# Fewer accumulating DMAs, later weight sums and other banks for two turns in a two-layer decoder kernel

## The chip, the cores and the metric

The kernel runs on one core of a Trainium2 chip. The metric is the time of one execution on the device in microseconds, here the median of several runs. A core has five engines that run beside each other: TensorE (PE in the profile, its weight loads PEld), VectorE (DVE), ScalarE (ACT), GpSimd (POOL) and SyncE (SP). Each works off its own queue of instructions in order; semaphores order the queues against each other. Sixteen DMA engines move data; DMAs are issued here from SP (plain loads) and from POOL (loads that add to what is there already, called accumulating).

## The reference

Two layers over 512 tokens of width 1024, all in float32. A layer is a half-weighted SwiGLU network, a mixer (windowed attention and a short convolution behind one projection), and another half-weighted SwiGLU network:

```python
def rms_norm(x, gain):
    inv = lax.rsqrt(jnp.mean(x * x, axis=-1, keepdims=True) + NORM_EPS)
    return x * inv * gain

def swiglu(h, w_gate, w_up, w_down):          # 1024 -> 2816 -> 1024
    return (jax.nn.silu(h @ w_gate) * (h @ w_up)) @ w_down

for l in range(2):
    x = x + 0.5 * swiglu(rms_norm(x, ffn1_norm[l]), ffn1_wg[l], ffn1_wu[l], ffn1_wd[l])
    h = rms_norm(x, mix_norm[l])
    z = h @ w_in[l]
    ...
    x = x + concat([attn_out, conv_out]) @ w_out[l]
    x = x + 0.5 * swiglu(rms_norm(x, ffn2_norm[l]), ffn2_wg[l], ffn2_wu[l], ffn2_wd[l])
return rms_norm(x, final_norm)
```

So there are four feed-forward networks in a run. The change touches them only.

## The kernel before

**Products in three parts.** Each operand of a product is split into a high part, rounded to a short float32 form (`fp32r`), and a low part, the rest: `wh`, `wl` for weights, `xh`, `xl` or `ah`, `al` for activations. A product is three matmuls for each piece: high x high, low x high, high x low.

**How a weight tile is split.** A tile (512 KB, 128 x 1024) is loaded by SP into one of 8 `raw` buffers (line 174), and then, by `split` (lines 189 to 191), ScalarE casts it to `wh` and VectorE makes `wl = raw - wh`. There is a second way, `"far"` (lines 224 to 228): ScalarE writes `wl = -raw` (L226) and casts `wh = raw` (L227) and a DMA from POOL's queue adds `raw` onto `wl`. Since `wl` and `wh` have three buffers each, a tile's split starts when the product three tiles before it is done. Splits are made in the order of the list `order`, two products ahead (`SPLIT_AHEAD`); `plan` fills that list, and a tile in it has a word for how it is made.

**A network's stages.** The 22 column tiles of the hidden width are taken in blocks of two. The lists `FIRST` (first network), `INNER` (the two in the middle) and `LAST` name the stages. In the last three:

- `("p", 0)`: block 0's two gate and two up tiles by plain products, 24 matmuls each (L255, L258, L262, function `plain`). All four tiles are `"far"` here.
- `("d", (0,))`: block 0's part of the down-projection, two tiles, 48 matmuls in all, `"far"` too.
- `("w", 1)`, `("w", 3)`, ...: a pair of blocks by `winograd2`, a product scheme with seven half-size products instead of eight. It works with sums of weight quarters, made in the buffers: for each of two halves `h` the tiles `a11`, `a12` are loaded, `s1` (`w_up`, two quarters added) and `s3` (`w_up` with `w_gate` added) are loaded with a second, accumulating DMA from POOL (L185), and `a22` is loaded. VectorE makes `s2 = a11 + s1` in `a11`'s buffer (L207) and the last chain's `s4 = a12 + a11` in `a12`'s buffer (L233). The seven chains (`CHAINS`) run in the order a11, a12, s2, s3, s1, a22, s4; each is 48 matmuls (L722), 24 for each half.
- `("d", ...)`: the down-projection of the blocks that are ready.

A chain that starts (`start`) takes two PSUM banks: `x` of the tag `mm` (4 banks), `w` of `aux` (2), `y` of `sc` (2). They are given out in turn. The steps 0, 2, 4 and 6 go to `x`, 1 to `w`, 3 and 5 to `y`.

**Turning.** `winograd2` leaves activations with tokens in the partitions; the down-projection wants them the other way, so four tiles for each pair are transposed on TensorE into a bank of the tag `sc` (L766), read by ScalarE (`ah`) and VectorE (`al`). These turns are kept in `pending` and made by `flush`: within the first three steps of a pair that follows directly, or between the products of a down-projection. A pair follows a pair directly only once in a network: `("w", 1)`, `("w", 3)` in the last three.

**What else VectorE does around block 0.** In the product before it (the mixer's output or a down-projection), VectorE adds each column to `x`, then makes `xl` (L374) and sums squares (L383). During block 0 it scales and sums the normed activations into the operands of the seven chains (`scale`, `make`: b11, b21, t1 to t4, b22).

The order of each engine's instructions is set by a scheduler that plans with costs of its own, not by the order in which the code is written alone.

Of the kernel before, what the change touches and what calls it, by code (L numbers as in the profile page):

```python
# [15 lines left out]
P = 128  # L16
D = 1024
S = 512
# [5 lines left out]
KC = D // P  # L24
NT = S // P
# [14 lines left out]
FORMS = ("a11", "a12", "s2", "s3", "s1", "a22", "s4")  # L40
# [15 lines left out]
def trunk_kernel(  # L56
# [32 lines left out]
    def psum(tag, shape, name):  # L89
        return ps.tile(shape, F32, tag=tag, bufs={"mm": 4, "sc": 2, "aux": 2}[tag], name=name)  # L90
# [69 lines left out]
    order = []  # L160
# [3 lines left out]
    def add_unit(*unit):  # L164
        units.append(unit)
        return len(units) - 1
# [26 lines left out]
    def need_split(g):  # L193
        while state["split"] <= min(g, len(order) - 1):
            n = state["split"]
            u, what = order[n]
            if what in (None, "wide", "far"):
                need_raw(u + LOAD_AHEAD)
                raw = raw_of.pop(u)
            elif isinstance(what, tuple):  # L200

                what, h = what
                last = {"a11": 0, "a12": 4, "s2": 2, "s3": 6, "s1": 2, "a22": 8, "s4": 4}[what]
                need_raw(u + max(last, 4) + h + LOAD_AHEAD)
                a11, s1, a12, s3, a22 = (raw_of.get(u + 2 * i + h) for i in range(5))
                if what == "s2":
                    nc.vector.tensor_add(a11, a11, s1)  # L207
                raw = {"a11": a11, "a12": a12, "s2": a11, "s3": s3, "s1": s1, "a22": a22, "s4": a12}[what]
            else:

                need_raw(u + 4 + LOAD_AHEAD)
                a11, a12, s1, s3, a22 = (raw_of.get(u + i) for i in range(5))
                if what == "s2":
                    nc.vector.tensor_add(a11, a11, s1)
                if what == "s4":
                    nc.vector.tensor_add(a11, a11, a12)
                raw = {"a11": a11, "a12": a12, "s2": a11, "s3": s3, "s1": s1, "a22": a22, "s4": a11}[what]
                if what == FORMS[-1]:
                    for i in range(5):
                        del raw_of[u + i]  # L220
            shape = list(raw.shape)
            hi = wpool.tile(shape, F32R, tag="wh", bufs=3, name=f"wh_{n}")
            lo = wpool.tile(shape, F32R, tag="wl", bufs=3, name=f"wl_{n}")
            if what == "far":

                nc.scalar.activation(lo, raw, AF.Copy, scale=-1.0)  # L226
                nc.scalar.copy(hi, raw)  # L227
                nc.gpsimd.dma_start(out=f32(lo), in_=raw, accum_op=ALU.add)
            elif n:
                split(hi, lo, raw)  # L230
            if isinstance(order[n][1], tuple):
                if what == "s2":
                    nc.vector.tensor_add(a12, a12, a11)  # L233
                done = {"s2": (0,), "s1": (1,), "s3": (3,), "a22": (4,), "s4": (2,)}.get(what, ())
                for i in done:
                    del raw_of[u + 2 * i + h]
            split_of[n] = (hi, lo)
            state["split"] += 1
# [42 lines left out]
    def plan():  # L281
        def cols(src, k0, kc, n, how=None):
            wide = abreast(kc)
            for b in range(0, n, wide):
                order.append((add_unit((src, k0, kc, b * P, wide * P)), how))

        def plain(wg, wu, b, how):
            for w in (wg, wu):
                for j in range(2):
                    order.append((add_unit((w, 0, KC, (2 * b + j) * P, P)), how))  # L290

        def up(wg, wu, b):
            top, low = ((w, k, KC // 2, 2 * b * P, 2 * P) for w, k in ((wu, 0), (wu, KC // 2)))
            first = (wg, 0, KC // 2, 2 * b * P, 2 * P)
            u = add_unit(first)
            add_unit((wg, KC // 2, KC // 2, 2 * b * P, 2 * P))
            add_unit(top, low)
            add_unit(top, first)
            add_unit(low)
            order.extend((u, what) for what in FORMS)  # L300

        def up2(wg, wu, b):
            def at(w, half, h):
                return w, KC // 2 * half + 2 * h, 2, 2 * b * P, S

            u = len(units)
            for what in (
                ((wg, 0),), ((wu, 0), (wu, 1)), ((wg, 1),), ((wu, 0), (wg, 0)), ((wu, 1),)
            ):
                for h in range(2):  # L310
                    add_unit(*(at(w, half, h) for w, half in what))
            order.extend((u, (what, h)) for what in FORMS for h in range(2))

        def ffn(wg, wu, wd, stages):
            for what, b in stages:
                how = "far" if b in (0, (0,)) and stages is not FIRST else None
                if what == "p":
                    plain(wg, wu, b, how)
                if what == "u":
                    up(wg, wu, b)  # L320
                if what == "w":
                    up2(wg, wu, b)
                if what != "d":
                    continue
                if stages is not LAST or b[-1] < FF // (2 * P) - 1:
                    cols(wd, 2 * b[0], 2 * len(b), KC, how)
                    continue
                for half in range(2):
                    for k in range(0, 2 * len(b), 2):
                        u = add_unit((wd, 2 * b[0] + k, 2, half * S, S))  # L330
                        if half == 0:
                            order.append((u, "wide"))

        for l in range(DEPTH):
            ffn(ffn1_wg[l], ffn1_wu[l], ffn1_wd[l], INNER if l else FIRST)
            for c in MIX_COLS:
                for j in range(2):
                    order.append((add_unit((w_in[l], 0, KC, (2 * c + j) * P, P)), None))
            cols(w_out[l], 0, KC, KC)
            ffn(ffn2_wg[l], ffn2_wu[l], ffn2_wd[l], INNER if l + 1 < DEPTH else LAST)  # L340
# [253 lines left out]
    def ffn(norm, stages, after=None, late=None):  # L594
# [4 lines left out]
        def plain(b):  # L599
            gates = []  # L600

            def gate(acc):
                t = g2(f"gate_{norm.i}_{b}_{len(gates)}")
                nc.vector.tensor_mul(t, acc, norm.inv)
                nc.scalar.activation(t, t, AF.Silu)
                nc.vector.tensor_mul(t, t, norm.inv)
                gates.append(t)

            hi, lo = g4(f"ah_{norm.i}_{b}"), g4(f"al_{norm.i}_{b}")

            def up(j, acc):
                t = gates[j]
                nc.vector.tensor_mul(t, acc, t)
                split(hi[:, j, :], lo[:, j, :], t)

            if norm.inv is None:
                accs = norm.groups(4, [opening] if first else [])
                gate(accs[0])
                gate(accs[1])
                norm.scale(stock if first else g4)  # L620
                up(0, accs[2])
                if not first:
                    norm.make("b11")
                up(1, accs[3])
            else:
                accs = [group(norm.h) for _ in range(2)]
                norm.make("b11")
                gate(accs[0])
                accs.append(group(norm.h))
                gate(accs[1])  # L630
                norm.make("b21")
                accs.append(group(norm.h))
                up(0, accs[2])
                norm.make("t2")
                up(1, accs[3])
            acts[b] = (hi, lo)
# [57 lines left out]
        def winograd2(b, between=None):  # L694


            name = f"{norm.i}_{b}"
# [9 lines left out]
            for step, (acc, operand, start) in enumerate(CHAINS):  # L707
# [41 lines left out]
                            nc.scalar.activation(gates[2 + u], out, AF.Silu)  # L749
                            nc.vector.tensor_mul(ups[2 + u], ups[2 + u], gates[2 + u])  # L750

                if step < 3:
                    flush(2 if step == 2 else 1)
                if between:
                    between(step)
                if not first and step < 3:
# [3 lines left out]
            for j in range(2):  # L760
                acts[b + j] = (g4(f"ah_{name}_{j}"), g4(f"al_{name}_{j}"))

            def turn(c):
                tp = psum("sc", [P, S], f"at_{name}_{c}")
                for t in range(NT):
                    nc.tensor.transpose(  # L766
                        tp[:, t * P : (t + 1) * P], ups[t][:, c * P : (c + 1) * P], ident
                    )
                hi, lo = acts[b + c // 2]
                split(hi[:, c % 2, :], lo[:, c % 2, :], tp)  # L770

            pending.extend(lambda c=c: turn(c) for c in range(NT))

        pending = []

        def flush(n=1):
            for _ in range(n):
                if pending:
                    pending.pop(0)()

        end = None
        for i, (what, b) in enumerate(stages):
# [392 lines left out]
```

## Time and profile before

| | |
|---|---|
| Runs | 1734.77, 1739.11, 1740.63 us; median 1739.11 |
| Profiled execution | 1734.7 us, its span 1732.7 us |
| TensorE's granted clock | 0.999 |
| TensorE busy | 1717.6 us (99%) |
| VectorE, ScalarE, GpSimd busy | 1217.9, 850.8, 164.4 us |
| HBM | 229.68 MB read, 2.10 MB written |

The profile is of one execution. Matmuls overlap in the pipe, so that a row's duration (0.39 us) is longer than the step from one start to the next; the step is what counts. In the timeline a row is: start, duration, engine, line, operation, out<-in, and in brackets the idle time before it with what ended it. In the views of waits a row is: who <- for whom: total, times, longest. The three networks with the stages above begin at about 520, 867 and 1376 us of the span.

### The profile page before, as it was taken

The numbers are of one execution on the slowest core, as the hardware profiler recorded it, in microseconds if no ns is written. First come the engines' busy times: TensorE is split into PE (matmuls) and PEld (weight loads), VectorE is DVE, ScalarE is ACT, GpSimd is POOL, SyncE is SP. The second block draws the span as 40 slices with busy tenths as digits, with TensorE's granted clock in tenths as the row PEclk, the third lists the DMA queues.
The fourth block names the chain that finished last, engine by engine and source line by source line (L and its number), as shares of the span: only waits on it lengthen the run. The fifth ranks groups of instructions, "written<-read, shape, count | busy, mean of one in ns | idle before, by whom it ended". The sixth has DMA issues, their size and how long they took to land.

```text
span 1732.7 us, 20824 instructions
## 1 busy us (share of the span) xinstructions
PE 1717.6 (99%) x7922; PEld 1416.9 (82%) x7922; DVE 1217.9 (70%) x1685; ACT 850.8 (49%) x1236; POOL 164.4 (9%) x151
## 2 busy tenths in 40 slices
PE   9999999999999999999999999999999999999998
PEld 7888888988887888888878888888888878888887
DVE  7986666668757966666688666666787498666763
ACT  6544443546545544444465444444564555344353
POOL 1011000001201110110011100100022011100101
PEclk9999999999999999999999999999999999999999
DMA  8467455422437674574377745743124567664541
GB/s 244 107 167 205 130 139 142 131 73 62 119 102 169 171 198 129 136 192 136 110 168 174 198 130 142 183 143 100 50 61 127 129 143 205 162 167 127 144 134 49
DMA packets 202503, 242.57 MB, mean 140 GB/s; under 512 B 7772, under 2 KB 125604, under 8 KB 202404
## 3 DMA queue, kind: packets, MB, share of 16 engines
q1 hardware_dynamic: 176932, 189.46, 35.9%
q0 software_dynamic: 24320, 50.34, 17.1%
q8 instruction: 62, 1.02, 0.2%
q10 hardware_dynamic: 1152, 1.45, 0.2%
q14 instruction: 37, 0.30, 0.1%
HBM read 229.68 MB, written 2.10 MB: 134 GB/s over the span
## 4 chain that ended last, share of the span: by engine, by line
PE 84%; issue 6%; DVE 5%; DMA 4%; ACT 1%; POOL 0%; SPq 0%; POOLq 0%; ACTq 0%; DVEq 0%
PE x L722 22%; PE acc L255 12%; PE acc L258 12%; PE acc L262 12%; PE y L722 12%; PE w L722 5%; DMA wl<-raw 3%; PE at L766 2%; DVE wl L191 2%; DMA raw<-in_ffn_wu_dram 1%; PE end L857 1%; PE end L859 1%; PE end L858 1%; PE x L666 1%; PE pt L1043 1%
## 5 line engine op out<-in xcount | busy, mean ns | idle before, releaser
L190 ACT CAST wh<-raw 128x1024 fp32r<-128x1024 f32 (+2 forms) x415 | 432.8, 1045 | 617.9 <-PE acc L258 219.3
L191 DVE TENSOR_TENSOR wl<-raw,wh 128x1024 fp32r<-128x1024 f32 (+2 forms) x414 | 507.3, 1227 | 231.6 <-ACT wh L190 230.4
L255 PE MATMUL acc<-ah,wh 128*128 128x512 f32 x640 | 254.1, 399 | 0.0
L262 PE MATMUL acc<-ah,wl 128*128 128x512 f32 x640 | 250.0, 391 | 0.0
L258 PE MATMUL acc<-al,wh 128*128 128x512 f32 x640 | 249.1, 389 | 0.0
L805 DVE SCALAR_TENSOR_TENSOR x<-acc,x 128x512 f32<-128x512 f32 x176 | 120.0, 688 | 108.1 <-PE acc L262 107.5
L255 PE MATMUL acc<-xh,wh 128*128 128x512 f32 x448 | 176.5, 394 | 0.1
L258 PE MATMUL acc<-xl,wh 128*128 128x512 f32 x448 | 175.2, 391 | 0.1
L262 PE MATMUL acc<-xh,wl 128*128 128x512 f32 x416 | 163.0, 392 | 5.4 <-DMA wl<-raw 5.4
L262 PEld LDWEIGHTS acc<-ah,wl 128*128 128x128 f32 x640 | 120.1, 188 | 26.0
L258 PEld LDWEIGHTS acc<-al,wh 128*128 128x128 f32 x640 | 120.4, 188 | 23.3
L255 PEld LDWEIGHTS acc<-ah,wh 128*128 128x128 f32 x640 | 120.0, 188 | 23.6 <-ACT ah L190 1.0
L185 POOL DMA_DIRECT2D raw<-in_ffn_wu_dram x39 | 47.1, 1211 | 671.5 <-DVE u L746 343.6
L258 PEld LDWEIGHTS acc<-xl,wh 128*128 128x128 f32 x448 | 84.2, 188 | 18.3 <-DVE xl L374 1.6
L255 PEld LDWEIGHTS acc<-xh,wh 128*128 128x128 f32 x448 | 84.2, 188 | 17.3 <-issue 0.5
L262 PEld LDWEIGHTS acc<-xh,wl 128*128 128x128 f32 x416 | 78.1, 188 | 23.4 <-DMA wl<-raw 7.1
L190 ACT CAST ah<-at 128x512 fp32r<-128x512 f32 x76 | 44.1, 584 | 67.6 <-PE at L766 67.6
L185 POOL DMA_DIRECT2D raw<-in_ffn_wg_dram x39 | 46.9, 1204 | 234.5 <-DMA raw<-in_ffn_wu_dram 153.4
L191 DVE TENSOR_TENSOR al<-at,ah 128x512 fp32r<-128x512 f32 x76 | 51.9, 687 | 15.2 <-ACT ah L190 15.0
L722 PE MATMUL x<-wh,ft1h 128*128 128x512 f32 x152 | 59.7, 392 | 0.2
L722 PE MATMUL y<-wh,ft3h 128*128 128x512 f32 x152 | 59.6, 392 | 0.3
L722 PE MATMUL x<-wh,ft2h 128*128 128x512 f32 x152 | 59.5, 392 | 0.0
(297 smaller groups left out, 3441.0 us busy)
## 6 DMA issues: line engine op xcount, KB each, us to landing
raw<-in_ffn_wu_dram SPq DMA_DIRECT2D x127, 512.0 KB, 3.8
raw<-in_ffn_wg_dram SPq DMA_DIRECT2D x87, 512.0 KB, 4.9
raw<-in_ffn_wd_dram SPq DMA_DIRECT2D x82, 512.0 KB, 3.4
raw<-in_ffn_wu_dram POOLq DMA_DIRECT2D x39, 512.0 KB, 7.6
raw<-in_ffn_wg_dram POOLq DMA_DIRECT2D x39, 512.0 KB, 6.0
raw<-in_w_in_dram SPq DMA_DIRECT2D x36, 512.0 KB, 3.7
wl<-raw POOLq DMA_DIRECT2D x18, 512.0 KB, 7.4
raw<-in_w_out_dram SPq DMA_DIRECT2D x16, 512.0 KB, 4.1
```

The costliest lines, as they stand in the source:

```text
L185: nc.gpsimd.dma_start(out=r, in_=rows_of(*more), accum_op=ALU.add)
L190: nc.scalar.copy(hi, raw)
L191: eng.tensor_sub(lo, raw, f32(hi))
L255: nc.tensor.matmul(acc, hi[:, k, :], rhs[k][0], start=k == 0, stop=False)
L258: nc.tensor.matmul(acc, hi[:, k, :], rhs[k][1], start=False, stop=n == 0 and k == last)
L262: nc.tensor.matmul(acc, lo[:, k, :], rhs[k][0], start=False, stop=k == last)
L666: nc.tensor.matmul(out, w[:, k, cols], x_[:, k, :], start=start and k + i == 0, stop=k == KC // 2 - 1 and i == 2, skip_group_check=not start,)
L722: nc.tensor.matmul(out, x_[:, 2 * h + k, tok], w[:, k, :], start=start and h + k + i == 0, stop=h + k == 2 and i == 2, skip_group_check=no ...
L766: nc.tensor.transpose(tp[:, t * P : (t + 1) * P], ups[t][:, c * P : (c + 1) * P], ident)
L805: nc.vector.scalar_tensor_tensor(xs[c], acc, 0.5, xs[c], op0=ALU.mult, op1=ALU.add)
L857: nc.tensor.matmul(acc, ah[:, tok], wh[:, cols], start=k == 0, stop=False)
L858: nc.tensor.matmul(acc, ah[:, tok], wl[:, cols], start=False, stop=False)
```

## The change

- Block 0's four gate and up tiles are no longer `"far"`: each is split by ScalarE and VectorE as other tiles are. Its two down-projection tiles stay `"far"`.
- In the first pair (`("w", 1)`) the first tile (`a11`, first half) becomes `"far"`.
- The sum `a12 + a11` is issued after the split of `s3` instead of that of `s2`, so `a11`'s buffer is given back there too.
- The two turns made at step 2 of a pair take banks of the tag `mm` instead of `sc`.

In all 18 accumulating DMAs `wl<-raw` become 9.

```diff
@@ need_split
             n = state["split"]
             u, what = order[n]
+            far = what == "far"
...
-                what, h = what
+                what, h, far = what
...
-            if what == "far":
+            if far:
 
                 nc.scalar.activation(lo, raw, AF.Copy, scale=-1.0)
                 nc.scalar.copy(hi, raw)
...
             if isinstance(order[n][1], tuple):
-                if what == "s2":
+                if what == "s3":
                     nc.vector.tensor_add(a12, a12, a11)
-                done = {"s2": (0,), "s1": (1,), "s3": (3,), "a22": (4,), "s4": (2,)}.get(what, ())
+                done = {"s3": (0, 3), "s1": (1,), "a22": (4,), "s4": (2,)}.get(what, ())
@@ plan
-        def plain(wg, wu, b, how):
+        def plain(wg, wu, b):
             for w in (wg, wu):
                 for j in range(2):
-                    order.append((add_unit((w, 0, KC, (2 * b + j) * P, P)), how))
+                    order.append((add_unit((w, 0, KC, (2 * b + j) * P, P)), None))
...
-        def up2(wg, wu, b):
+        def up2(wg, wu, b, far):
...
-            order.extend((u, (what, h)) for what in FORMS for h in range(2))
+            order.extend(
+                (u, (what, h, far and what == "a11" and h == 0)) for what in FORMS for h in range(2)
+            )
...
-                how = "far" if b in (0, (0,)) and stages is not FIRST else None
+                how = "far" if b == (0,) and stages is not FIRST else None
...
-                    up2(wg, wu, b)
+                    up2(wg, wu, b, b == 1)
@@ winograd2
-                if step < 3:
-                    flush(2 if step == 2 else 1)
+                if step < 2:
+                    flush()
+                if step == 2:
+                    flush(2, "mm")
...
-            def turn(c):
-                tp = psum("sc", [P, S], f"at_{name}_{c}")
+            def turn(c, tag="sc"):
+                tp = psum(tag, [P, S], f"at_{name}_{c}")
...
-            pending.extend(lambda c=c: turn(c) for c in range(NT))
+            pending.extend(lambda *tag, c=c: turn(c, *tag) for c in range(NT))
...
-        def flush(n=1):
+        def flush(n=1, *tag):
             for _ in range(n):
                 if pending:
-                    pending.pop(0)()
+                    pending.pop(0)(*tag)
```

## The prediction

> **What bounds the kernel now.** I read the page first, then TensorE's view of waits, then the timeline around each wait.
>
> ```profile
> span 1732.7 us, 20824 instructions
> PE 1717.6 (99%) x7922; PEld 1416.9 (82%) x7922; DVE 1217.9 (70%) x1685; ACT 850.8 (49%) x1236; POOL 164.4 (9%) x151
> ...
> raw<-in_ffn_wu_dram SPq DMA_DIRECT2D x127, 512.0 KB, 3.8
> ...
> wl<-raw POOLq DMA_DIRECT2D x18, 512.0 KB, 7.4
> ```
>
> TensorE (PE) is busy for 99% of the span and the change leaves its work alone, so the only time to win is time in which TensorE stands still or runs stretched. The chain of waits gives the pace of an undisturbed stretch:
>
> ```profile
> 660.12 5.44 PE x L722 x24
> ```
>
> That is 5.44 / 24 = 0.227 us for one matmul of 512 columns; a longer step between two starts is a loss. TensorE's waits, summed over the run:
>
> ```profile
> PE acc L262 <- DMA wl<-raw: 5.4, 3, 2.5
> ...
> PE y L722 <- DVE wl L191: 0.5, 3, 0.2
> ```
>
> Both come three times, once in each of the three feed-forward networks after the first. One is at the last product of block 0's gate and up tiles, which waits for the low part `wl` that an accumulating DMA makes. The other is in the first pair's fourth chain (`y`, weights `s3`). The timeline of TensorE shows the first at its largest:
>
> ```profile
> 537.57 0.39 PE L258 MATMUL acc<-xl,wh 128*128 128x512 f32 x1
> 540.43 0.50 PE L262 MATMUL acc<-xh,wl 128*128 128x512 f32 x1 [2.47 <-DMA wl<-raw]
> 540.77 0.40 PE L255 MATMUL acc<-xh,wh 128*128 128x512 f32 x1
> ```
>
> The start comes 2.86 us after the one before, 2.63 over the pace: 0.16 more than the view's 2.47, and the step behind it (0.34) loses another 0.11. So a wait costs what the view says plus 0.27.
>
> **Block 0's four tiles lose their accumulating DMAs.** Why that DMA is late is in the timelines of GpSimd (POOL) and SyncE:
>
> ```profile
> 530.27 1.20 POOL L185 DMA_DIRECT2D raw<-in_ffn_wu_dram  x1 [6.63 <-DMA raw<-in_ffn_wu_dram]
> 530.99 1.40 POOL L228 DMA_DIRECT2D wl<-raw  x1
> 534.14 0.85 POOL L228 DMA_DIRECT2D wl<-raw  x1 [1.75 <-ACT wl L226]
> ...
> 549.32 1.20 POOL L185 DMA_DIRECT2D raw<-in_ffn_wg_dram  x1 [8.53 <-DMA raw<-in_ffn_wu_dram]
> ```
>
> ```profile
> 543.68 0.37 SPq L174 DMA_DIRECT2D raw<-in_ffn_wu_dram  x1
> ```
>
> ```profile
> DMA to landing us min/median/max: 4.4/7.4/9.5
> ```
>
> POOL's queue is first in, first out. The fourth tile's `wl` DMA stood behind an accumulating load of `w_up` that itself waited 6.63 us for its base load, and then took 9.4 us (530.99 to 540.4). The base load was late because its buffer was still being read by an earlier `wl` DMA. After the change the four tiles are split by a ScalarE cast and a VectorE subtraction, and their raw buffers come free when that subtraction ends instead of when a DMA lands. The wait goes: 5.4 + 3 x 0.27 = 6.2 us.
>
> What this adds is 12 subtractions on VectorE, and what it takes away is 12 negated copies on ScalarE:
>
> ```profile
> 521.40 1.05 ACT L226 ACTIVATE wl<-raw 128x1024 fp32r<-128x1024 f32 x1
> ```
>
> ```profile
> 523.10 0.75 DVE L374 SCALAR_TENSOR_TENSOR xl<-x,par,xh 128x512 fp32r<-128x512 f32 x1 [1.74 <-ACT xh L373]
> ```
>
> In the order of instructions each subtraction stands just ahead of an `xl`, during the product before block 0. There VectorE idles 1.74 us waiting for ScalarE's `xh`, and that `xh` now comes about 1 us sooner because the 1.05 us copy ahead of it is gone. A subtraction (1.22 us, row 565.30 below) fits the gap; cost taken as nothing. If the gap were full, `xl` of the last column would be late; the one above ends at 523.85, and TensorE needs it 21 matmuls (4.8 us) into the next product, at about 525.2: 1.4 us of cover.
>
> **The first pair's first tile and its sums.** One tile in each network goes the other way: its subtraction leaves VectorE for an accumulating DMA. And the sum `a12 + a11`, for the last chain, moves behind the split of `s3`. VectorE's timeline:
>
> ```profile
> 545.75 0.69 DVE L613 TENSOR_TENSOR gate<-acc,gate 128x512 f32<-128x512 f32 x1 [2.71 <-PE acc L262]
> ...
> 565.30 1.22 DVE L233 TENSOR_TENSOR raw<-raw,raw 128x1024 f32<-128x1024 f32 x1
> ...
> 569.31 1.21 DVE L233 TENSOR_TENSOR raw<-raw,raw 128x1024 f32<-128x1024 f32 x1
> ```
>
> From 545.75 VectorE runs without a gap until 580, so everything in its queue up to there is late by what stands ahead of it. The row's 2.71 us of idle shows that it had been waiting for TensorE's stalled product, so it moves forward with it. The stalls it causes are these:
>
> ```profile
> 570.99 0.39 PE L722 MATMUL x<-wh,ft2l 128*128 128x512 f32 x1
> 571.48 0.50 PE L722 MATMUL y<-wh,ft3h 128*128 128x512 f32 x1
> ...
> 574.11 0.39 PE L722 MATMUL y<-wh,ft3l 128*128 128x512 f32 x1
> 574.65 0.50 PE L722 MATMUL y<-wl,ft3h 128*128 128x512 f32 x1 [0.16 <-DVE wl L191]
> ```
>
> 0.49 and 0.54 instead of 0.227, with 0.11 after each: 0.79 us, three times, 2.4 us. The `wl` in question will come 1.2 (the removed subtraction) + 2.4 (two sums) = 3.6 us sooner, well over the lateness. What is late next is `wl` of the fifth chain (`s1`), behind the same sums: only the 1.2 helps it, while TensorE arrives 0.8 sooner. Bounds are 0 and 0.7 us for each network; I take 0.2, near zero because that chain does not wait now: 0.6 us in all. In the other pairs the order of instructions leaves the sums where they were. In the first pair `a22`'s load, which takes `a11`'s buffer, starts later; the page's 3.8 us for such a load stand against four products (4 x 2.72 us) from the split of `s3` to that of `a22`, so I take nothing.
>
> The moved tile's DMA is the part with a price I cannot read off. ScalarE can start its cast only when the fourth tile's product ends (call this T; about 542.8 without the stall), and needs 2.1 us for cast and negated copy; POOL issues it at T + 2.3. The 4.4 to 9.5 us above put the landing at T + 6.7 to T + 11.8. TensorE needs it after block 0's 48 matmuls of down-projection and two of its own: T + 50 x 0.227 = T + 11.4. So cost is 0 to 0.4 us each; I take 0, since the queue is emptier (four fewer such DMAs ahead). The Trainium skill, page "DMA: Bandwidth & Descriptors", section "Anatomy of one DMA — SWDGE (gpsimd) path", fits 2.0 us plus bytes over 436 GB/s; for 512 KB that is an estimate of 3.2 us, by which the cost would be 0 as well, though this trace's minimum is already 4.4.
>
> **Turns through other banks.** When the second pair runs its third chain, the last two transposed tiles of the first pair are turned in the two `sc` banks that the next chain's `y` needs. The order of instructions therefore puts part of the fifth chain first, whose weights are not ready:
>
> ```profile
> 613.57 0.38 PE L766 MATMUL at<-ident,p 128*128 128x128 f32 x2
> 614.03 0.50 PE L722 MATMUL x<-wh,ft1h 128*128 128x512 f32 x1
> ...
> 614.85 0.39 PE L722 MATMUL x<-wh,ft1l 128*128 128x512 f32 x1
> 615.29 0.50 PE L722 MATMUL x<-wl,ft1h 128*128 128x512 f32 x1
> ```
>
> ```profile
> 959.28 0.50 PE L722 MATMUL x<-wh,ft1h 128*128 128x512 f32 x1
> ```
>
> ```profile
> 1469.13 0.50 PE L722 MATMUL x<-wh,ft1h 128*128 128x512 f32 x1
> ```
>
> Two small transposes take 0.22 us, so 0.46 loses 0.24; 0.44 loses 0.21; with 0.11 after each it is 0.67 us, and the other two rows show the same stretched matmul in the other networks: 2.0 us. With `mm` banks `y` comes first, its banks long free. In exchange the next down-projection takes the bank of the pair's own `x` accumulator:
>
> ```profile
> 635.13 0.60 ACT L749 ACTIVATE gate<-x 128x512 f32<-128x512 f32 x1 [0.53 <-PE x L722]
> ```
>
> ```profile
> 636.29 0.39 PE L255 MATMUL acc<-ah,wh 128*128 128x512 f32 x1
> ```
>
> ScalarE is done reading it at 635.73, 0.56 us before the first matmul that would reuse it. Cost nothing; if ScalarE slipped by a whole cast (1.05 us) it would be 0.5 us for each network.
>
> **Sum.** 6.2 + 2.4 + 2.0 - 0.6 = 10.0 us. The profiled execution took 1734.7 us (span 1732.7), so it would become 1724.7. The median of the three runs, 1739.1, lies 4.4 above it; off the median the forecast is 1729.1 us. A difference under 0.3% (5.2 us) can hardly be told from none here.
>
> **Rivals.** (1) POOL's queue holds the moved tile back. In the new order its DMA stands behind the accumulating load of row 549.32, which needs a base load, which needs the buffer of block 0's first down-projection tile (still an accumulating DMA: issued 534.14, buffer free at 543.68). I count on that DMA landing by about 539, alone in the queue. If it keeps its 9.5 us, the load is issued as before at 549.3, the tile's DMA at 550.5, and with 7.4 to 9.5 us it lands at 557.9 to 560.0 against a need at 554.2: 3.7 to 5.8 us for each network, 11 to 17 in all, 1740 to 1746 us. It decides from a landing about 2 us later than I count on. For it: all six `wl` DMAs were slow. Against: what crowded them is what the change removes. Chance 0.11, about half of it slower by over 0.3%.
> (2) VectorE becomes the bound ahead of block 0: four subtractions (4.9 us) against 1.4 us of cover leave up to 3.5 us for each network if none of them finds a gap, 10.5 in all: 1740 us, just above the time before. Against: its idle gaps there, 1.74 us in one column. Chance 0.08.
> (3) The moved tile's DMA is written out late because VectorE is full while GpSimd prepares it: one subtraction of 1.22 us in the way, on top of the 0.4 above, 1.6 each, 4.8 in all, 1734 us. Row 549.32 speaks against: 1.20 us in the midst of the full stretch, like 530.27 before it. The Trainium skill, page "SBUF — State Buffer", section "SBUF: two separate sides", has this rule: a VectorE instruction holding the shared port keeps GpSimd from writing descriptors. Chance 0.04.
> (4) The change does not do what it says on VectorE and the banks: the two shorter waits only move to the next chain, and just 6.2 us go: 1733 us. Chance 0.05.
>
> **How the numbers follow.** The forecast has 0.72. Its own range runs from 1722 (the fastest run, 1734.8, less 10.6 and some 2 us of DMA waits in the other runs that this profile doesn't show) to 1733 (the slowest, 1740.6, less 7.6). To 1738 it takes in cases 3 and 4 and most of 2. Faster by over 0.3%: 0.72 + 0.05 + 0.03 = 0.80; same: 0.05 + 0.06 + 0.01 = 0.12; slower: 0.06 + 0.02 = 0.08.
>
> **What would show it.** Right: no wait of TensorE on `wl<-raw` at L263 (L262 of the code before); VectorE 14 us busier at most; the first pair's chains back to 5.44 us for 24; after the turns 0.227 from the first `y`. Wrong: TensorE waiting at the first pair's first matmuls (`x<-wl,fb11h`) on a DMA says case 1 or 3; waiting for `xl` in block 0's first product says case 2; a wait of the down-projection behind the second pair on ScalarE's `gate` says that the banks only moved the stall.

## The result, and the profile after

The changed kernel takes **1724.0 us** (median of six runs, 1723.67 to 1724.62) against 1739.7 us for six runs of the kernel before beside it (1734.77 to 1742.1). The ratio is 0.9913, 95% interval 0.9899 to 0.9926: faster by 0.9%. The forecast was 1729.1 with a range of 1722 to 1738: the measured time lies inside it, near its lower end. The profiled execution took 1723.67 us, 11.0 less than the one of before; the sum had said 10.0.

From the page of the kernel after:

```profile
span 1721.9 us, 20808 instructions
PE 1713.1 (99%) x7922; PEld 1418.3 (82%) x7922; DVE 1229.7 (71%) x1694; ACT 844.2 (49%) x1227; POOL 156.6 (9%) x142
...
PE 97%; DVE 2%; ACT 1%; issue 0%; ACTq 0%; DVEq 0%
...
wl<-raw POOLq DMA_DIRECT2D x9, 512.0 KB, 5.3
```

VectorE has 11.8 us more to do and ScalarE 6.6 less; neither bounds the kernel, since the chain that ended last (third line) is now TensorE for 97%, where it was 84%. The nine accumulating DMAs `wl<-raw` that are left land in 5.3 us at the median, instead of 7.4. All that TensorE waited for, by its view of waits:

```profile
PE idle L117 <- DVE warm L486: 1.2, 1, 1.2
PE o L1063 <- DVE pl L1052: 0.8, 2, 0.4
PE acc L256 <- ACT ah L190: 0.2, 1, 0.2
```

The first two belong to the kernel's start and the mixer; the third is taken up further down. No row names `wl<-raw`, none names `y`. The chain of waits shows the first four of the first pair's seven chains. Each is 24 matmuls, 12 for each half of its weights (the description of `winograd2` above gives 48 and 24, which is twice too many):

```profile
554.28 5.56 PE x L725 x24
559.84 5.44 PE w L725 x24
565.28 5.44 PE x L725 x24
570.72 5.44 PE y L725 x24
```

The fourth, where `y` stalled before, runs at 5.44 us, the undisturbed pace; the first is 0.12 over it, and that is where the moved tile is needed. The turns, in TensorE's timeline:

```profile
610.25 0.38 PE L771 MATMUL at<-ident,p 128*128 128x128 f32 x2
610.39 0.48 PE L725 MATMUL y<-wh,ft3h 128*128 128x512 f32 x1
610.70 0.40 PE L725 MATMUL y<-wh,ft3l 128*128 128x512 f32 x1
610.94 0.39 PE L725 MATMUL y<-wl,ft3h 128*128 128x512 f32 x1
```

`y` follows the transposes at once: 0.14 after the last two, then steps of 0.31 and 0.24. The first of these loses 0.09 us, where 0.67 was lost before.

**One sum for each profiled execution.** I took each step between two starts of TensorE's matmuls over the whole run, subtracted the undisturbed step of its size (0.227 us for 512 columns, 0.120 for 256, 0.109 for less) and added up what is left. This is the time lost by waits, by stretched steps, and at half clock:

| profiled execution of | lost steps, us | time, us | difference |
|---|---|---|---|
| before, first | 24.0 | 1734.70 | 1710.7 |
| before, again | 28.5 | 1739.26 | 1710.8 |
| after | 13.2 | 1723.67 | 1710.5 |
| tiles only | 18.6 | 1729.11 | 1710.5 |
| no block-0 change, no moved tile | 23.6 | 1734.17 | 1710.6 |
| no block-0 change | 30.1 | 1740.78 | 1710.7 |
| no accumulating DMA | 20.7 | 1731.26 | 1710.5 |

The kernels have the same matmuls, so the difference can only change with what lies ahead of the first matmul, behind the last, or outside the span; it is the same to 0.3 us. The sum is bookkeeping and names no cause, but it says where to look: each loss stands between two rows of TensorE. Over the last three networks together, lost steps fall from 6.6 to 0.0 us around the end of block 0's gate and up products, from 2.7 to 0.2 in the first pair and from 2.4 to 0.3 in the second pair with its turns, and rise from 0.6 to 1.0 in block 0's part of the down-projection. That is all of the 10.8 us between the first row and the third.

### The profile page after: what moved, and what is told of

Its sections match the earlier page's. It is cut to its first block, busy times and chain, and to the rows that moved or that the text cites. A ratio compares the mean times of both kernels' runs of the same rounds, so it can differ in the third digit from the quotient of the medians.

```text
span 1721.9 us, 20808 instructions
## 1 busy us (share of the span) xinstructions
PE 1713.1 (99%) x7922; PEld 1418.3 (82%) x7922; DVE 1229.7 (71%) x1694; ACT 844.2 (49%) x1227; POOL 156.6 (9%) x142
## 3 DMA queue, kind: packets, MB, share of 16 engines
q8 instruction: 62, 1.02, 0.2%
## 4 chain that ended last, share of the span: by engine, by line
PE 97%; DVE 2%; ACT 1%; issue 0%; ACTq 0%; DVEq 0%
PE x L725 24%; PE acc L256 15%; PE acc L259 15%; PE acc L263 15%; PE y L725 12%; PE w L725 6%; PE at L771 2%; PE end L864 1%; PE end L862 1%; PE end L863 1%; PE x L669 1%; PE pt L1048 1%; DVE p L1041 0%; DVE wl L191 0%; ACT p L1033 0%; PE y L669 0%
## 5 line engine op out<-in xcount | busy, mean ns | idle before, releaser
L190 ACT CAST wh<-raw 128x1024 fp32r<-128x1024 f32 (+2 forms) x424 | 443.0, 1045 | 616.1 <-PE acc L259 243.1
L191 DVE TENSOR_TENSOR wl<-raw,wh 128x1024 fp32r<-128x1024 f32 (+2 forms) x423 | 518.5, 1227 | 232.7 <-ACT wh L190 231.5
L725 PE MATMUL w<-wh,fb21h 128*128 128x512 f32 x152 | 59.5, 392 | 0.0
```

The costliest lines, as they stand in the source:

```text
L191: eng.tensor_sub(lo, raw, f32(hi))
L725: nc.tensor.matmul(out, x_[:, 2 * h + k, tok], w[:, k, :], start=start and h + k + i == 0, stop=h + k == 2 and i == 2, skip_group_check=no ...
```

## The experiments

Theory A: the gain is the removal of stalls of TensorE in three places (block 0's waits for accumulating DMAs, the first pair's fourth chain, the turns), and the spread of the kernel before is the landing time of those DMAs. Its rivals: the waits only move; the moved tile is held back in GpSimd's queue; of the edits to the pair only one does the work; the spread comes from elsewhere.

### The kernel before, once more

No edit; a second profile, to see what the spread of the runs is made of.

> The kernel before, profiled once more. Theory A (the accumulating DMAs' landing varies from execution to execution, and this is what spreads the runs of before over 7 us): if the execution takes more than 1734.7 us, TensorE's waits for wl<-raw at L262 sum to more than 5.4 us by about the difference, while the waits of the y chain (0.8 us a network) and behind the turns (0.7 us a network) stay. Theory B (the spread lies elsewhere: start, mixer, a clock): the waits for wl<-raw stay at 5 to 6 us whatever the time.

It took 1739.26 us. TensorE's waits:

```profile
PE acc L262 <- DMA wl<-raw: 8.3, 3, 3.7
...
PE y L722 <- DVE wl L191: 0.2, 1, 0.2
```

The waits for the DMAs are 2.9 us longer than in the first profile, and time is 4.56 longer. The remaining part lies behind the longest wait (timeline of TensorE, then the windows behind it, whose last three columns are granted clock, DMA share and GB/s):

```profile
541.59 0.58 PE L262 MATMUL acc<-xh,wl 128*128 128x512 f32 x1 [3.66 <-DMA wl<-raw]
541.97 0.63 PE L255 MATMUL acc<-xh,wh 128*128 128x512 f32 x1
542.39 0.63 PE L258 MATMUL acc<-xl,wh 128*128 128x512 f32 x1
...
1399.97 0.50 PE L262 MATMUL acc<-xh,wl 128*128 128x512 f32 x1 [2.98 <-DMA wl<-raw]
1400.30 0.39 PE L255 MATMUL acc<-xh,wh 128*128 128x512 f32 x1
```

```profile
541.50:543.50 2.00, 1.91 (x5) 1.54 (x6) 1.60 (x3) 0.36 (x1) 0.00 (x0) 0.59 1.05 207
543.50:545.50 2.00, 2.00 (x6) 1.55 (x6) 0.00 (x0) 0.00 (x0) 0.00 (x0) 0.55 1.02 268
545.50:548.00 2.50, 2.50 (x13) 2.04 (x12) 0.00 (x0) 0.00 (x0) 0.00 (x0) 1.00 0.86 295
```

Behind 3.66 us of idle TensorE runs at steps of 0.43 instead of 0.227 us until 545.3, for 3.8 us. The granted clock is 0.59 and 0.55 in the first two windows, which reach a little over the edges of the slow stretch; from 541.9 to 545.2 it is 0.50. Behind 2.98 us nothing of the kind is seen. So a DMA that is late enough was paid for twice here: by the wait, and by the slow steps behind it. The Trainium skill, page "TensorE: Matmul & The Clock Gate", section "What's actually happening", says that a gate lets through only half the clock after an idle window of about 3.4 us; the trace agrees, with 2.98 us on the one side and 3.66 us on the other.

### Block 0's tiles alone

The kernel before, with this edit only:

```diff
-                how = "far" if b in (0, (0,)) and stages is not FIRST else None
+                how = "far" if b == (0,) and stages is not FIRST else None
```

> Only block 0's four gate and up tiles are split by ScalarE and VectorE; the sums, the turns and the first pair stay as before. Theory A: no wait of TensorE on wl<-raw, y and turn stalls as before, so the time after plus 2.4 plus 2.0, 1728.4 us, in a spread of about 1 us. Theory B: the median falls by the 6.2 us of the profile alone, to 1733.5 us, and the spread stays near 7 us. Rival of the prediction (VectorE becomes the bound ahead of block 0): a wait for xl in block 0's first product, and more than 1731 us.

1728.58 us (six runs, 1728.07 to 1729.11) against 1738.28 for the kernel before (1732.58 to 1743.0); ratio 0.9953, 0.9936 to 0.9971. Its waits, but for those at the start and in the mixer:

```profile
PE y L722 <- DVE wl L191: 0.5, 3, 0.2
PE w L722 <- DVE wl L191: 0.3, 1, 0.3
PE acc L255 <- ACT ah L190: 0.2, 1, 0.2
```

No wait for a DMA is left, while `y` still waits three times, as before. The spread falls with this edit alone to 1.0 us, from 10.4 in 23 runs of the kernel before (7.3 in the six beside the changed kernel): it was these DMAs and what follows from them. This one line of the change is 9.7 us at the medians, and the time is that of theory A (1728.4).

### The rest, with block 0 untouched

Later sums and other banks, with block 0's four tiles by accumulating DMAs as before; first without the moved tile, then with it (the changed kernel less the block-0 edit).

> The other edits without block 0's tiles and without the moved tile: later sums and mm banks only; block 0's tiles keep their accumulating DMAs. Theory A: 4.4 us less than before in the median (about 1735.3 us), with the spread of before, and waits on wl<-raw of 5 us and more. Theory B: most of the 15.7 us, to about 1729 us, with a narrow spread.

1733.22 us (12 runs, 1728.61 to 1741.66), ratio 0.9974 (0.9958 to 0.9990).

```profile
PE acc L263 <- DMA wl<-raw: 6.2, 3, 3.8
```

> The kernel after with block 0's four tiles on accumulating DMAs as before: the moved tile of the first pair now stands in GpSimd's crowded queue. By the prediction's first rival its DMA is issued at about 7 us after the end of block 0's last gate and up product and lands later than needed: waits of TensorE on wl<-raw at the first pair's first chain (x<-wl,fb11h) of 1 to 4 us a network on top of those in block 0, in all 1737 to 1746 us. If the queue does not matter for it: as the run with the other edits alone, about 1735 us, and no such wait.

1737.57 us (12 runs, 1732.39 to 1740.78), ratio 1.0002 (0.9990 to 1.0014).

```profile
PE acc L263 <- DMA wl<-raw: 9.8, 3, 4.7
...
PE x L725 <- DMA wl<-raw: 1.2, 1, 1.2
```

Both keep the spread and the waits. The second row of the second kernel is rival 1 of the prediction, seen here: the moved tile comes too late in one network of three, by 1.2 us. More is lost in block 0 itself: of its three waits in that execution, those of 4.75 and 3.76 us are followed by half clock, as the 3.8 us one in the first kernel is. So the moved tile on top of block 0's four DMAs takes back, at the medians, 4.4 of the 5.1 us that the other two edits win; the moved tile and the edit to block 0 belong together. Why block 0's own waits grow with the moved tile (its DMA comes behind them in the queue) is not settled: each is one profile, though the medians differ the same way.

### The pair's tile by engines; the sum early; neither

Three kernels from the changed one: its first pair's first tile split by engines again; its sum back behind `s2`; both.

```diff
-                    up2(wg, wu, b, b == 1)
+                    up2(wg, wu, b, False)
```

> The kernel after, with the first pair's first tile split by ScalarE and VectorE again. By the prediction VectorE's queue is 1.2 us later in the first pair: the y chain's weights still come in time (2.4 us from the sums remain), the s1 weights come up to 0.7 us late, and ScalarE's negated copy no longer stands ahead of ah (0.2 to 0.5 us a network come back): 1722.5 to 1726 us. Rival (the moved tile, not the sums, frees the y chain): the y stalls are back, 1726.4 us.

```diff
-                if what == "s3":
+                if what == "s2":
...
-                done = {"s3": (0, 3), "s1": (1,), "a22": (4,), "s4": (2,)}.get(what, ())
+                done = {"s2": (0,), "s1": (1,), "s3": (3,), "a22": (4,), "s4": (2,)}.get(what, ())
```

> The kernel after, with the sum a12 + a11 made with s2 again. By the prediction the y chain's weights are 2.4 us later than in the kernel after and still 1.2 us earlier than before: part of the 0.8 us a network comes back, 1724.5 to 1726.4 us. Rival (the moved tile alone suffices): no stall in the first pair, 1724.0 us.

> The kernel after, with the first pair's first tile split by ScalarE and VectorE and the sum a12 + a11 again behind the split of s2: the corner that is missing beside the kernel after (1724.0), the one with the tile by engines (1724.9) and the one with the sum early (1724.2). If the two edits add up, it is 1724.0 + 0.9 + 0.2 = 1725.1 us and the wait of y on wl in the fourth chain of the first pair stays away. If either of them alone is enough and neither is not (the theory from the two runs before), the three waits of about 0.2 us on wl (y of the fourth chain) come back with their stretched steps: 2.4 us over the kernel after, 1726.4 us.

| median, us (six runs: range) | sum late | sum early |
|---|---|---|
| tile by accumulating DMA | 1724.01 (1723.67 to 1724.62) | 1724.16 (1723.66 to 1725.21) |
| tile by engines | 1724.86 (1724.60 to 1725.63) | 1725.88 (1725.68 to 1726.48) |

Only where both are undone do the waits of `y` come back; in the view of waits two of them are long enough to be listed, and the timeline shows one of the three stretched steps:

```profile
PE y L725 <- DVE wl L191: 0.3, 2, 0.2
```

```profile
571.34 0.39 PE L725 MATMUL y<-wh,ft3l 128*128 128x512 f32 x1
571.89 0.50 PE L725 MATMUL y<-wl,ft3h 128*128 128x512 f32 x1 [0.16 <-DVE wl L191]
```

With the tile by engines, the late sum is worth 1.0 us (1725.88 to 1724.86); with the moved tile, 0.15, less than the ranges. Either edit takes VectorE out of the way of the fourth chain. With the late sum alone, a stall stands elsewhere (TensorE's timeline of the kernel with the tile by engines and the late sum):

```profile
576.32 0.39 PE L725 MATMUL x<-wh,ft1l 128*128 128x512 f32 x1
576.76 0.50 PE L725 MATMUL y<-wh,ft4h 128*128 128x512 f32 x1
```

TensorE's order puts the start of the sixth chain amid the fifth, and it comes 0.22 us late with 0.11 behind it, once in each network: 1.0 us, about the difference to the changed kernel (0.85). The four medians come from three sessions, so differences well under 1 us rest on the steps. In the first pairs of all three networks these lose 0.2 us (both edits), 1.1 (moved tile alone), 1.3 (late sum alone) and 2.7 (neither). About half of the 1.1 is not VectorE's: there the moved tile's own DMA lands too late. The prediction added up 1.2 and 2.4 us of relief; each of the two stalls was only about 0.3 us late, so that each edit alone all but removed them.

### The turns in `sc`

```diff
-                    flush(2, "mm")
+                    flush(2)
```

> The kernel after, with the two turns in sc banks as before; only TensorE's order differs, at three places. By the prediction 0.7 us a network come back in the same two steps behind the turns: 1726.0 us. Rival (the stall came from weights that were late for other reasons, gone now): 1724.0 us.

1726.25 us (1726.0 to 1726.81), 2.2 over the changed kernel; ratio to the kernel before 0.9930 (0.9916 to 0.9944). The stall stands where it stood in TensorE's timeline:

```profile
609.95 0.38 PE L771 MATMUL at<-ident,p 128*128 128x128 f32 x2
610.41 0.50 PE L725 MATMUL x<-wh,ft1h 128*128 128x512 f32 x1
...
611.67 0.50 PE L725 MATMUL x<-wl,ft1h 128*128 128x512 f32 x1
```

In this execution, the slowest of the six, the moved tile's DMA also lands late in the third network, 10.0 us after its issue:

```profile
1404.96 0.50 PE L725 MATMUL x<-wl,fb11h 128*128 128x512 f32 x1 [0.65 <-DMA wl<-raw]
```

### No accumulating DMA at all

The down-projection's two tiles and the pair's first tile by engines too:

```diff
-                how = "far" if b == (0,) and stages is not FIRST else None
+                how = None
...
-                    up2(wg, wu, b, b == 1)
+                    up2(wg, wu, b, False)
```

> The kernel after with no accumulating DMA for a low part at all: block 0's down-projection tiles and the first pair's first tile are split by ScalarE and VectorE too. By the prediction VectorE, full from the end of block 0's products on, gets three more subtractions of 1.2 us in each network; what does not fit makes weights of the first pair late: 1 to 3 us a network, 1727 to 1733 us, with waits of TensorE on wl from VectorE. Rival (an accumulating DMA always costs more than a subtraction): 1724 us or less.

1730.91 us (1730.71 to 1731.26), ratio 0.9957 (0.9943 to 0.9971): 6.1 us slower than the kernel that differs only in the down-projection's two tiles (1724.86). The wait, and the timelines of VectorE and ScalarE ahead of it:

```profile
PE acc L256 <- ACT ah L190: 4.4, 3, 1.5
```

```profile
538.86 1.21 DVE L191 TENSOR_TENSOR wl<-raw,wh 128x1024 fp32r<-128x1024 f32 x1
...
541.98 0.68 DVE L616 TENSOR_TENSOR gate<-acc,gate 128x512 f32<-128x512 f32 x1
```

```profile
542.84 1.04 ACT L190 CAST wh<-raw 128x1024 fp32r<-128x1024 f32 x1 [3.77 <-issue]
543.79 0.61 ACT L190 CAST ah<-gate 128x512 fp32r<-128x512 f32 x1
```

TensorE needs the first `ah` of the down-projection at 542.8 and gets it at 544.4. With the two subtractions ahead of it (the later one is shown) VectorE starts the first `gate` at 541.98, where the kernel that keeps the two DMAs starts it at 539.50; and in the order that follows, ScalarE casts the next weight tile ahead of `ah`. So the time lies in the 1727 to 1733 us that were expected, but not for the reason expected: most of the loss (5.5 of 6.6 us in lost steps) is at activations, which share the two engines with the weights; only about 1 us is in the first pair. That is why these two tiles in each network are better left to the slow DMA.

### Idle matmuls inside the wait

The kernel before, with six matmuls of zeros in front of the matmul that waits for block 0's fourth `wl` (the trace lists five of the six, 1.24 us).

```diff
+            if fill and k == 0:
+                spin(fill, acc_fill(n))
             if n != 0 and not late:
...
+                        fill=6 if self.i and n == 4 and len(accs) == 3 else 0,
```

> The kernel before, with six idle matmuls of zeros (about 1.3 us) on TensorE just before the matmul of block 0's fourth gate/up product that waits for the accumulating DMA, in the last three networks; their result is used by nothing. They stand inside a wait that is 2.5 to 3.7 us long, so they cost nothing there. If the clock halves behind a long wait because TensorE has stood idle for more than about 3 us, then the wait in the trace shrinks to 1.2 to 2.4 us, the granted clock of the 4 us behind it is 1.00 in all three networks, and executions that had a 3.7 us wait save 4 us x 0.45 = 1.8 us each: the median comes down by 1 to 3 us and the slowest runs most (spread under 5 us). If the slow stretch comes from something else (the DMA load, the moment), the clock stays near 0.55 behind the wait where the DMA lands late, and the median does not move (within 1 us of the kernel before). Where a wait is shorter than 1.3 us the fillers cost up to 1.3 us each.

1732.49 us (12 runs, 1730.3 to 1735.91) against 1737.2 (17 runs, 1733.29 to 1745.39); ratio 0.9974 (0.9958 to 0.9989). In the third network the DMA is as late as where the clock fell in the kernel before: from the start of the last matmul of the product to that of the waiting one it is 4.15 us (1391.26 to 1395.41), there 4.05 (537.54 to 541.59). TensorE's timeline and the windows:

```profile
1391.26 0.39 PE L258 MATMUL acc<-xl,wh 128*128 128x512 f32 x1
1391.71 1.24 PE L117 MATMUL fill<-zero 128*128 128x512 bf16 x5
1395.41 0.50 PE L264 MATMUL acc<-xh,wl 128*128 128x512 f32 x1 [2.45 <-DMA wl<-raw]
```

```profile
1395.40:1397.40 2.00, 1.99 (x9) 1.63 (x10) 2.00 (x5) 0.17 (x1) 0.00 (x0) 1.00 1.06 209
1397.40:1399.40 2.00, 2.00 (x10) 1.67 (x9) 1.21 (x3) 0.00 (x0) 0.00 (x0) 1.00 1.01 298
```

The clock stays at 1.00, with the DMA engines as busy (share 1.06 and 1.01) as behind the 3.66 us wait (1.05 and 1.02): what halves it is idle time of TensorE, not the late DMA. That is one place in one trace, but the granted clock on record for each run says the same. Of the 17 runs of the kernel before, the eight with a clock of 0.999 or more took 1733.3 to 1737.2 us, the seven with 0.997 or 0.998 took 1736.1 to 1739.9, and the two with 0.995 took 1744.4 and 1745.4; with the fillers eleven of twelve runs have 0.999 or more. So the spread of the kernel before goes with half clock.

The median can't be laid to the clock alone: the fillers also changed the scheduler's order on VectorE, and the waits of `y` (2.4 us by the prediction's rows) are gone from this trace. The median comes down by 4.7 us, more than the 1 to 3 expected; less the 2.4, about 2.3 are left for the clock, which this run does not show by themselves. The spread, 5.6 us, is about half of before (12.1), where less than 5 was expected.

## Why the prediction was right, and where it was off

**Block 0's waits (6.2 us).** Right in place and size for the profiled execution: no such wait is left, and the 6.6 us of lost steps in that stretch are gone. The one-edit kernel loses 5.4 us less between matmuls in all (24.0 to 18.6), since it loses some elsewhere: 0.9 us more around a new wait at `w` in one network, and 0.3 at an `ah`. VectorE took the four subtractions without delaying `xl`, as said: rival 2 fell, and VectorE's busy time grew by 11.8 us of the 14 allowed.

**Down to the median (the term that was mis-sized).** The prediction carried the 4.4 us between profile and median over to the changed kernel, as if it were a property of the measurement. It was the same DMA waits, longer than in the profiled execution, and half clock behind them: the second profile shows both, and for the runs without a profile the granted clock says it. With them gone, profile and median agree (1723.67 and 1724.01). Taken out of the profile, the sum gave 1724.7; that, and not 1729.1, was the right forecast for the median. The prediction's own-range argument had the beginning of this ("some 2 us of DMA waits in the other runs"), but used it for the lower end only.

**The first pair (2.4 us, less 0.6).** The stalls went, and were worth 1.9 us at the medians (1725.88 to 1724.01), 2.2 in lost steps of the whole run (15.4 to 13.2, the 15.4 by the same sum). The reason given was too generous: either edit nearly suffices. The lateness of `s1`'s weights that was charged at 0.6 didn't come; the fifth chain waits nowhere in the trace of the changed kernel. That is most of the 1.0 us between the sum and the measured 11.0.

**The moved tile's DMA (nothing).** Right in its result, wrong in its reason, and so in part luck. GpSimd's timeline of the kernel after:

```profile
534.15 0.90 POOL L229 DMA_DIRECT2D wl<-raw  x1 [9.03 <-ACT wl L227]
...
542.97 1.20 POOL L185 DMA_DIRECT2D raw<-in_ffn_wg_dram  x1 [2.54 <-DMA raw<-in_ffn_wu_dram]
545.32 0.89 POOL L229 DMA_DIRECT2D wl<-raw  x1 [1.15 <-ACT wl L227]
```

Block 0's first down-projection DMA (534.15) landed at 538.6, where the prediction counted on about 539; so the base load behind it and the accumulating load of 542.97 came in time, and rival 1 was off. But the tile's own DMA, issued 545.32, landed at 554.51, after 9.2 us: the late end of the 4.4 to 9.5 that was allowed for. The matmul that needs it starts at 554.57, on its pace, and the step behind it loses 0.09. In the other networks it took 8.9 and 8.8 us. The prediction took nothing because the queue would be emptier; but in the three traces that have this tile and no DMA for block 0's four, it took 8.6 to 10.0 us in all nine cases, longer than the 7.4 us median of before. There is no slack: in the kernel with the turns in `sc` it was 0.65 us late in one network, in the one with the sum early 0.15, and with block 0's DMAs kept 1.2. So the cost is nothing to some 0.9 us for an execution, with the slower step behind the wait. The mechanism of rival 1 did not come, since the loads ahead were in time. Its argument that all six `wl` DMAs of a network were slow was misread, though: in the kernel before the first of each six, alone in the queue, landed after 4.4 us, and the second after 5.2 to 6.3.

**The turns (2.0 us).** Measured 2.2 when undone. The down-projection behind the second pair doesn't wait for the banks.

**What was not foreseen.** In the first of the three networks the down-projection's second activation is late; ScalarE has the moved tile's cast and negated copy ahead of it (chain of waits of the kernel after).

```profile
543.01 1.05 ACT wh L228
544.07 0.96 ACT wl L227
545.02 0.51 ACT ah L190
545.58 0.97 PE acc L256 x3
```

It costs 0.5 us there, and 0.2 in each of the other two networks. VectorE had written its `gate` by 543.6. The moved tile is hardly the cause, though: the kernel before loses 0.2 us at this place in each network, and the three kernels with block 0's edit and the tile by engines (that edit alone, the tile by engines, neither edit to the pair) lose the same 0.5 in the first network and 0.2 in the others. What grows, 0.3 us in the first network, comes with block 0's edit; why only there stays open.

Rivals 3 and 4 fell: GpSimd's issue took 0.89 us in the midst of VectorE's full stretch, and the two shorter waits left no successor.

## What to carry to other kernels

When the runs of a kernel spread (here by 0.6%) and a profile shows waits for DMAs, ask whether the spread itself is made of these waits: profile a second run, and compare the granted clock of each run with its time. A change that removes the waits can then bring the time below the fastest run so far, by more than one profile shows. A DMA chosen to relieve an engine is paid for by its landing time at its worst; compare that with the need before counting the engine's microsecond, and keep it where the engine's queue is the tighter of the two. Where two edits relieve the same queue by more than the lateness, undo each alone and then both before crediting either.

## What the hardware showed

TensorE's clock fell to half (granted 0.50) around the end of each of four waits, of 3.66, 3.76, 3.80 and 4.75 us; it did so at no wait of 2.98 us or less. The slow steps went on for 3.2 to 3.8 us behind the first three, and for 5.3 us behind the longest. In the 3.76 us case they begin about 1 us after the wait's end (TensorE's timeline of the kernel with block 0 untouched and the moved tile):

```profile
892.27 0.50 PE L263 MATMUL acc<-xh,wl 128*128 128x512 f32 x1 [3.76 <-DMA wl<-raw]
...
893.30 0.61 PE L256 MATMUL acc<-xh,wh 128*128 128x512 f32 x1
```

An accumulating DMA of 512 KB within the core took from 4.4 us, alone in its queue, to 10.9 us (issued 534.85, landed 545.74 in the same kernel) when others stood beside it.
